# Gate, values and the second half of the output projection with 512 weight columns per matmul instead of 256

## The chip, the cores and the metric

The kernel runs on one core of a Trainium2 chip. The metric is the device time of one execution in microseconds (us), as the median of several runs; all inputs and weights are float32 in device memory. One execution was also taken by the hardware profiler; its rows are what this document reads. Engines are named as in the profile: PE is TensorE's matmul, PEld its load of the stationary operand, DVE is VectorE, ACT ScalarE, POOL GpSimd, SP SyncE, which issues most DMAs.

## What is computed

Two decoder layers on 512 tokens of width 1024. Each layer projects the tokens once, runs two groups of heads side by side, maps both back, adds the residual and normalises, and then runs a gated feed-forward net in the same way. What matters here is the mixer:

```python
proj = x @ w_in[l]
hq, hf, hi, hg, nq, kc, vc, ks, vs, kw, vw, gt = split(proj)
o_a = hgrn2_mixer(hq, hf, hi, hg, ...)      # 4 heads of 128; hi: values, hg: output gate
o_b = nsa_mixer(nq, kc, vc, ks, vs, kw, vw, gt, ...)   # 8 attention heads of 64
mix = concatenate([o_a, o_b], -1) @ w_out[l]
x = layer_norm(ALPHA * x + mix, ln1_g[l], ln1_b[l])
```

In the recurrence `o_a` is a triangular combination of the values of all tokens, normalised per head and multiplied by `hg * sigmoid(hg)`. Values and gate are 512 columns each. The output projection has 1024 rows: the first 512 take `o_a`, the second 512 take `o_b`.

## The kernel before

**Products.** A float32 product is made of three matmuls (`mm3`, L78 to L83): each operand is split into a high part and a rest, and high x high, high x rest and rest x high are summed in a PSUM bank of 512 columns. `load_w` (L53 to L76) fetches a weight of 128x1024 through one of two raw buffers, converts it to the high part on ScalarE (L74) and forms the rest on VectorE (L75). The parts go into pairs of buffers (`wh`, `wl`, three of each), or, by a tag, elsewhere (`a`: one of eleven large buffers).

**Two shapes.** A projection whose result is wanted with features on the partitions (`feats`, L176) has the weight stationary and streams 512 tokens. Gate, values and the output projection are wanted with tokens on the partitions: there the tokens are stationary and the weight columns stream. The first half of the output projection and the down projection do this with 512 columns per matmul, one token tile of 128 to a bank (`wide_mm`, L215). Gate, values and the second half do it with 256 columns, two token tiles to a bank (`tok_mm`, L199); a matmul that opens the second tile of a bank is tied behind the one that opens the bank.

**Gate and values.** `tok256` (L767) makes one quarter of these 1024 columns: two banks with tag `d` (there are two such banks), two weights of 4 k-tiles by 256 columns, and for each of 8 k-tiles and 4 token tiles one `mm3`. ScalarE then copies values (L778), or forms the sigmoid of the gate (L785), which VectorE multiplies by the gate itself (L786). `G` and `V` are large buffers that hold the results.

**The order.** Around the change the order is written out by hand. `layer` first projects what heads 0 and 1 of the recurrence need, then the keys; after these comes the first half of the gate (`tok(1, 0)`, L894 and L895, columns 0 to 255), then the q projections of the first attention heads. Then `nsa_all` runs 16 steps, two for each attention head. After some steps it calls hooks (L898 to L908), whose work gets a priority a little behind the step: projections for heads 2 and 3, the recurrence's levels (`rec`), the second half of the gate after step 4 (`tok(1, 1)`), the values after steps 6 and 7 (`tok(0, 0)`, `tok(0, 1)`), the four outputs of the recurrence (`hg_out`, L426) after step 9, the first half of the output projection after 11 and 12, and the start of the second half after 15. The list scheduler that builds the program fixes each engine's order from priorities and a modelled timeline, so TensorE's queue holds matmuls of these hooks between those of the heads.

**Head outputs.** `hg_out` needs the values of all tokens and works through the single bank with tag `h`: matmuls (L439), squares, norm and gate, transposes (L451). The results are rows 0 to 3 of `Y`, the left operand of the first half (`first_half`, L867), whose result with the residual goes into the rows `R`. Attention heads fill rows 4 to 7 of `Y`.

**The second half.** `second_half` (L884) loads four weights, one for each quarter of 256 output columns, and starts three quarters of the first two token tiles with k 4 to 6. The rest follows after the attention (L921 to L928): for each pair of token tiles and each quarter the last k-tiles, the add onto the rows (L927) and `bn_stats` of 256 columns for each tile (L865). After each pair `norm_turn` normalises the rows and transposes them (L735) for the feed-forward net.

Of the kernel before, what the change touches and what calls it, by code (L numbers as in the profile page):

```python
# [12 lines left out]
AF = mybir.ActivationFunctionType  # L13
OP = mybir.AluOpType
# [20 lines left out]
class Kern:  # L35
# [162 lines left out]

    def tok_mm(self, pts, w, xs, ks, k0, k1, halves=((0, 1),)):  # L199

        for hs in halves:
            for k in ks:
                for t in [2 * h + e for h in hs for e in range(2)]:
                    wh, wl = w(k % 4 * 256, 256)

                    m = self.mm3(pts[t // 2][:, (t % 2) * 256:(t % 2 + 1) * 256], *xs(k, t), wh, wl,
                                 k == k0 and t % 2 == 0, k == k1 and t % 2 == 1)
                    if k == k0:
                        if t % 2 == 0:
                            first = m  # L210
                        else:
                            self.tc.add_manual_dep(m.ins, first.ins.name, mybir.DependencyInfo(
                                mybir.DependencyClass.NoSync, mybir.DependencyReason.DATA), reason="bank start")
# [539 lines left out]
    def layer(self, l):  # L753
# [21 lines left out]
        def take_v(q):  # L775
            def f(b, p):
                with tc.high_priority(offset=500):
                    nc.scalar.copy(self.V[:, 2 * b:2 * b + 2, q * 256:(q + 1) * 256], p)  # L778
            return f

        def take_g(q):
            def f(b, p):
                o = self.G[:, 2 * b:2 * b + 2, q * 256:(q + 1) * 256]
                with tc.high_priority(offset=500):
                    nc.scalar.activation(o, p, AF.Sigmoid)  # L785
                    nc.vector.tensor_tensor(o, p, o, op=OP.mult)  # L786
            return f
# [31 lines left out]
        def tok(which, q):  # L819
            return lambda: tok256(io["wt"][l, which, q], (take_v, take_g)[which](q))  # L820
# [32 lines left out]
        def quart(b, q):  # L853
            return R[b].rearrange("p a b -> p (a b)").rearrange("p (t c) -> p t c", c=1024)[:, :, q * 256:(q + 1) * 256]

# [4 lines left out]
        def v2(p):  # L860
            return p.rearrange("p (t c) -> p t c", c=256)

        def stats(b, q):
            for t in (2 * b, 2 * b + 1):
                nc.vector.bn_stats(self.stats[t][:, q * 6:(q + 1) * 6], rows[t][:, q * 256:(q + 1) * 256])  # L865
# [18 lines left out]
        def second_half():  # L884

            self.stats = [self.small(24, "st", tag="s") for _ in range(NT)]
# [237 lines left out]
def layout(inp):  # L1124
    f = {k: np.asarray(v) for k, v in inp.items()}
    L = DEPTH
# [8 lines left out]
    def tok(m):  # L1135

        k, n = m.shape[1] // 128, m.shape[2] // 256
        return m.reshape(L, k, 128, n, 256).transpose(0, 3, 2, 1, 4).reshape(L, n, 128, k * 256)
# [57 lines left out]
```

## Time and profile before

| | us |
|---|---|
| median of 3 runs | 1354.79 |
| lowest and highest | 1354.45, 1357.82 |
| the profiled execution | 1357.27 |
| its span, first to last instruction | 1355.5 |
| PE busy in the span | 1322.2 |
| DVE busy | 938.9 |
| ACT busy | 718.5 |

The busy time of an engine is the union of its rows. PE's rows overlap, since a matmul starts while the one before is still in the array; what a matmul costs a full queue is the time from its start to the next start. In layer 0 the stretch of the change lies between 76 and 327 us of the span, in layer 1 between 746 and 996. A line number is that of the printed kernel; where a helper issues an operation the line is the helper's, and the names behind it (out<-in) tell whose it is: `ps_d<-whi,xh` with 256 columns is `tok256`, `ps_d<-xh,whi` a projection with the weight stationary.

### The profile page before, as it was taken

The page shows a single profiled execution, that of the slowest core. Times are in us where ns is not written, and L with a number is a line of the kernel's source. Part 1 is how long each engine was busy: PE and PEld are TensorE (multiplying, and loading weights), DVE is VectorE, ACT ScalarE, POOL GpSimd, SP SyncE. Part 2 cuts the span into 40 slices and gives each one's busy share as a digit, 9 for nine tenths or more (in the row PEclk, how much of TensorE's full clock was granted, in tenths as well). Part 3 has the DMA queues.
Part 4 walks back from the last instruction along what each step waited for, and adds up shares of the span by engine and source line. Part 5 has one row for each costly group of instructions (what it writes and reads, how often), then busy time and mean ns, then how long its engine had stood idle before and what let it go on. Part 6 is the DMA issues. An engine that isn't in the chain of part 4 may idle for free.

```text
span 1355.5 us, 23189 instructions
## 1 busy us (share of the span) xinstructions
PE 1322.2 (98%) x8853; PEld 1212.5 (89%) x8853; DVE 938.9 (69%) x1914; ACT 718.5 (53%) x1460; POOL 158.6 (12%) x232
## 2 busy tenths in 40 slices
PE   8999999899999999999999999998999999999996
PEld 6988999789999999888899989987899999998885
DVE  4755898866887777624469468988559777775355
ACT  5254777745565555522543558778265655564131
POOL 1140111110011111000011001111000211100001
PEclk9999999999999999999999999999999999999999
DMA  7252213252177776334534122132513787754344
GB/s 235 79 164 101 78 56 101 55 146 91 63 174 191 180 182 171 102 107 151 191 122 129 65 86 75 55 106 73 154 47 102 181 192 181 181 131 140 94 143 152
DMA packets 61775, 170.26 MB, mean 126 GB/s; under 512 B 7519, under 2 KB 7695, under 8 KB 61152
## 3 DMA queue, kind: packets, MB, share of 16 engines
q1 hardware_dynamic: 44928, 128.93, 29.9%
q0 software_dynamic: 15728, 38.02, 13.4%
q10 hardware_dynamic: 1008, 1.84, 0.4%
q8 instruction: 69, 1.13, 0.3%
q14 instruction: 42, 0.34, 0.1%
HBM read 164.51 MB, written 7.10 MB: 127 GB/s over the span
## 4 chain that ended last, share of the span: by engine, by line
PE 88%; ACT 4%; DMA 3%; DVE 3%; issue 1%; POOL 0%; POOLq 0%; DVEq 0%; ACTq 0%; SPq 0%
PE ps_d L80 16%; PE ps_d L81 15%; PE ps_d L82 15%; PE ps_t L81 4%; PE ps_t L82 4%; PE ps_t L80 4%; PE ps_s L82 4%; PE ps_s L81 4%; PE ps_s L80 4%; PE ps_t L639 2%; DMA wraw<-in_wo 2%; PE ps_h L384 1%; PE ps_o L650 1%; PE ps_o L82 1%; PE ps_o L81 1%; PE ps_o L80 1%
## 5 line engine op out<-in xcount | busy, mean ns | idle before, releaser
L75 DVE TENSOR_TENSOR wlo<-wraw,whi 128x1024 fp32r<-128x1024 f32 (+1 forms) x122 | 149.0, 1221 | 158.2 <-ACT whi L74 157.7
L74 ACT CAST whi<-wraw 128x1024 fp32r<-128x1024 f32 (+1 forms) x122 | 127.5, 1045 | 227.4 <-PE ps_t L82 70.1
L80 PE MATMUL ps_d<-xh,whi 128*128 128x512 f32 (+1 forms) x456 | 154.1, 341 | 3.1 <-ACT gates L490 2.9
L112 ACT CAST whi<-wraw 128x512 fp32r<-128x512 f32 x144 | 89.0, 621 | 124.3 <-PE ps_d L81 93.9
L82 PE MATMUL ps_d<-xh,wlo 128*128 128x512 f32 (+1 forms) x456 | 154.6, 340 | 0.0
L81 PE MATMUL ps_d<-xl,whi 128*128 128x512 f32 (+1 forms) x456 | 154.2, 339 | 0.0
L113 DVE TENSOR_TENSOR wlo<-wraw,whi 128x512 fp32r<-128x512 f32 x144 | 98.4, 689 | 43.4 <-ACT whi L112 39.7
L81 PE MATMUL ps_d<-tl,whi 128*128 128x256 f32 x432 | 121.5, 283 | 0.0
L82 PE MATMUL ps_d<-th,wlo 128*128 128x256 f32 x432 | 120.5, 283 | 0.0
L80 PE MATMUL ps_d<-th,whi 128*128 128x256 f32 x432 | 120.3, 283 | 0.0
L80 PEld LDWEIGHTS ps_d<-xh,whi 128*128 128x128 f32 x456 | 85.8, 190 | 12.3 <-ACT gates L490 3.3
L82 PEld LDWEIGHTS ps_d<-xh,wlo 128*128 128x128 f32 x456 | 86.5, 190 | 8.8
L81 PEld LDWEIGHTS ps_d<-xl,whi 128*128 128x128 f32 x456 | 86.5, 190 | 8.3
L80 PE MATMUL ps_d<-whi,xh 128*128 128x256 f32 (+1 forms) x304 | 90.2, 298 | 0.0
L81 PE MATMUL ps_d<-wlo,xh 128*128 128x256 f32 (+1 forms) x304 | 88.4, 291 | 0.0
L82 PE MATMUL ps_d<-whi,xl 128*128 128x256 f32 (+1 forms) x304 | 87.3, 288 | 0.0
L81 PEld LDWEIGHTS ps_d<-tl,whi 128*128 128x128 f32 x432 | 82.9, 192 | 0.2
L80 PEld LDWEIGHTS ps_d<-th,whi 128*128 128x128 f32 x432 | 82.2, 192 | 0.2
L82 PEld LDWEIGHTS ps_d<-th,wlo 128*128 128x128 f32 x432 | 82.3, 192 | 0.0
L600 ACT ACTIVATE e<-e,mn 128x128 f32<-128x128 f32 (+3 forms) x128 | 71.6, 560 | 13.2 <-DVE mn L598 12.6
L598 DVE CUSTOM_DVE_ANT_0 e<-ps_s,strip 128x128 f32<-128x128 f32 (+3 forms) x128 | 59.2, 484 | 6.8 <-PE ps_s L613 5.9
L643 ACT CAST pth<-ps_t 128x384 fp32r<-128x384 f32 (+1 forms) x96 | 48.8, 510 | 25.9 <-PE ps_t L639 20.8
(482 smaller groups left out, 3957.7 us busy)
## 6 DMA issues: line engine op xcount, KB each, us to landing
wraw<-in_wd SPq DMA_DIRECT2D x59, 512.0 KB, 3.5
wraw<-in_wf SPq DMA_DIRECT2D x31, 512.0 KB, 3.3
wraw<-in_wg SPq DMA_DIRECT2D x26, 512.0 KB, 4.5
wraw<-in_wu SPq DMA_DIRECT2D x26, 512.0 KB, 4.1
ws<-in_wg SPq DMA_DIRECT2D x36, 256.0 KB, 3.5
ws<-in_wg POOLq DMA_DIRECT2D x36, 256.0 KB, 5.2
ws<-in_wu SPq DMA_DIRECT2D x36, 256.0 KB, 3.4
ws<-in_wu POOLq DMA_DIRECT2D x36, 256.0 KB, 4.6
```

Source lines behind the costliest of these rows:

```text
L74: nc.scalar.copy(h, raw[:, i:i + n])
L75: nc.vector.tensor_tensor(o, raw[:, i:i + n], h.bitcast(F32), op=OP.subtract)
L80: first = t.matmul(out, ah, bh, start=start, stop=False, **kw)
L81: t.matmul(out, ah, bl, start=False, stop=False, **kw)
L82: t.matmul(out, al, bh, start=False, stop=stop, **kw)
L112: nc.scalar.copy(h, raw)
L113: nc.vector.tensor_tensor(o, raw, h.bitcast(F32), op=OP.subtract)
L384: nc.tensor.matmul(p2[:, i], S[:, blk(i)], kq(128 * (i + 2), [[2 * w, n], [256 + w, 2], [1, w]]), start=True, stop=True)
L598: nc.vector.tensor_tensor_reduce(out=e, in0=pa, in1=st[:, 512 - pa.shape[-1]:], scale=1.0, scalar=3e38, op0=OP.add, op1=OP.min, accum_out=mn)
L600: nc.scalar.activation(e, e, AF.Exp, bias=mn, scale=-1.0, accum_out=sm)
L639: nc.tensor.transpose(p[:, c:c + 128], E[qt][:, j * 128:(j + 1) * 128], self.ident)
L643: nc.scalar.copy(ph[:, :c], p[:, :c])
```

## The change

`tok256` becomes `tok512`: one call makes all 512 columns of the gate, or of the values. It goes in two passes of two token tiles, each tile with a bank of its own. In the first pass it loads four weights of 2 k-tiles by 512 columns (the first into a large buffer with tag `a`, the other three into the `wh`/`wl` pairs) and uses each for two k-tiles and two token tiles; the second pass uses the same four weights for the other two tiles. With the last weight the tiles go one after the other (`by_tile`). Each tile is then copied, or passed through sigmoid and product, for itself. The whole gate comes after step 4, the whole values after step 6; nothing of the gate stands ahead of the q projections any more. The second half of the output projection has four weights of 2 k-tiles by 512 columns in the same buffers, one token tile to a bank, the add and one `bn_stats` of 512 columns for each tile and half. The weights are laid out for this on the host before the launch.

```diff
-        def tok256(src, consume):
-            pts = [self.ps("d") for _ in range(2)]
-            for i in range(2):
-                w = self.load_w(src[i])
-                self.tok_mm(pts, w, self.xs_of(x), [4 * i + a for a in range(4)], 0, NK - 1, ((0,), (1,)))
+        def tok512(src, consume):
+            ws = []
             for b in range(2):
-                consume(b, pts[b].rearrange("p (t c) -> p t c", c=256))
+                pts = {t: self.ps("d") for t in (2 * b, 2 * b + 1)}
+                for i in range(4):
+                    if b == 0:
+                        ws.append(self.load_w(src[i], tag=None if i else "a"))
+                    self.wide_mm(pts, ws[i], self.xs_of(x), i, i == 0, i == 3, i == 3)
+                for t, p in pts.items():
+                    consume(t, p)
...
+        def take_v(t, p):
+            with tc.high_priority(offset=500):
+                nc.scalar.copy(self.V[:, t], p)
+
+        def take_g(t, p):
+            with tc.high_priority(offset=500):
+                nc.scalar.activation(self.G[:, t], p, AF.Sigmoid)
+                nc.vector.tensor_tensor(self.G[:, t], p, self.G[:, t], op=OP.mult)
...
+        def second_mm(p, c, t, ks):
+            for k in ks:
+                self.mm3(p, *ysf(k, t), *self.wo[c][k // 2 - 2](k % 2 * 512, 512), k == 4, k == 7)
...
-            self.wo = [self.load_w(io["wo"][l, q, 0], tag=t) for q, t in enumerate((("at", 8), ("at", 8), ("f", 3), None))]
-            for q, tag in enumerate("ddh"):
-                early[q] = {0: self.ps(tag)}
-                self.tok_mm(early[q], self.wo[q], ysf, range(4, 7), 4, 7, ((0,),))
+            tags = ((("at", 8), ("at", 8)), (("f", 3), None))
+            self.wo = [[self.load_w(io["wo"][l, c, i], tag=tags[c][i]) for i in range(2)] for c in range(2)]
+            for c, t, tag in ((0, 0, "d"), (0, 1, "d"), (1, 0, "h")):
+                early[c, t] = self.ps(tag)
+                second_mm(early[c, t], c, t, range(4, 7))
...
-        alloc("G")()
-        tok(1, 0)()
         self.feats([feat("nq0"), feat("nq1")], x, lambda i, pt: self.take_q(i, pt))
...
-            4: [(0, rec(3)), (80, tok(1, 1))],
-            6: [(80, nq(3)), (80, alloc("V")), (80, tok(0, 0))],
-            7: [(80, tok(0, 1))],
+            4: [(0, rec(3)), (80, alloc("G")), (80, tok(1))],
+            6: [(80, nq(3)), (80, alloc("V")), (80, tok(0))],
...
-            for q in range(4):
-                pts = early.pop(q, None) if b == 0 else None
-                ks = range(4, 8) if pts is None else [7]
-                pts = pts or {b: self.ps("ddsd"[q] if b else "d")}
-                self.tok_mm(pts, self.wo[q], ysf, ks, 4, 7, ((b,),))
-                nc.vector.tensor_tensor(quart(b, q), v2(pts[b]), quart(b, q), op=OP.add)
-                stats(b, q)
+            for c in range(2):
+                for t in (2 * b, 2 * b + 1):
+                    p = early.pop((c, t), None)
+                    if p is None:
+                        p = self.ps("s" if c else "d")
+                        second_mm(p, c, t, range(4, 8))
+                    else:
+                        second_mm(p, c, t, [7])
+                    o = rows[t][:, c * 512:(c + 1) * 512]
+                    nc.vector.tensor_tensor(o, p, o, op=OP.add)
+                    nc.vector.bn_stats(self.stats[t][:, c * 6:(c + 1) * 6], o)
```

## Rows read from the trace of the kernel before

**Rows 1.** The page: busy time of the engines, granted TensorE clock, last chain by engine.

```profile
PE 1322.2 (98%) x8853; PEld 1212.5 (89%) x8853; DVE 938.9 (69%) x1914; ACT 718.5 (53%) x1460; POOL 158.6 (12%) x232
...
PEclk9999999999999999999999999999999999999999
...
PE 88%; ACT 4%; DMA 3%; DVE 3%; issue 1%; POOL 0%; POOLq 0%; DVEq 0%; ACTq 0%; SPq 0%
```

**Rows 2.** Groups by line and shape, TensorE: count | busy us, mean ns | idle before.

```profile
L80 PE MATMUL ps_d<-whi,xh 128*128 128x256 f32 x256 | 75.5, 296 | 0.0
```

**Rows 3.** Timeline, TensorE, first gate stage: start us, us, instruction.

```profile
89.08 0.28 PE L82 MATMUL ps_d<-whi,xl 128*128 128x256 f32 x1
...
92.44 0.28 PE L80 MATMUL ps_d<-whi,xh 128*128 128x256 f32 x1
```

**Rows 4.** Timeline, TensorE, q projection right behind it.

```profile
103.12 0.39 PE L82 MATMUL ps_d<-xh,wlo 128*128 128x512 f32 x1
...
106.52 0.39 PE L82 MATMUL ps_d<-xh,wlo 128*128 128x512 f32 x1
```

**Rows 5.** Windows: us; busy PE, PEld, DVE, ACT, POOL; clock, DMA share, GB/s.

```profile
148.00:173.00 25.00, 25.00 (x191) 24.12 (x191) 22.84 (x63) 19.74 (x48) 2.96 (x6) 1.00 0.17 54
207.00:230.00 23.00, 23.00 (x185) 22.34 (x184) 21.33 (x64) 16.28 (x40) 1.08 (x2) 1.00 0.23 70
230.00:256.00 26.00, 23.89 (x143) 19.97 (x143) 20.65 (x68) 20.92 (x65) 5.91 (x9) 0.93 0.35 112
256.00:283.00 27.00, 24.47 (x167) 21.60 (x167) 23.88 (x69) 20.41 (x59) 4.55 (x5) 1.00 0.30 73
301.00:327.00 26.00, 24.71 (x203) 23.98 (x201) 19.39 (x41) 11.54 (x17) 1.13 (x2) 1.00 0.37 118
899.00:925.00 26.00, 23.05 (x150) 19.02 (x148) 20.80 (x69) 21.58 (x66) 5.90 (x9) 1.00 0.35 112
925.00:952.00 27.00, 24.47 (x166) 21.64 (x167) 23.86 (x70) 20.48 (x60) 3.89 (x4) 1.00 0.29 69
```

**Rows 6.** Groups by line and shape, VectorE and ScalarE: columns as in rows 2.

```profile
L865 DVE BATCH_NORM_STATS2 st<-r 128x6 f32<-128x256 f32 x32 | 12.0, 416 | 0.1
L1057 DVE BATCH_NORM_STATS2 st<-r 128x6 f32<-128x512 f32 x16 | 10.6, 687 | 0.1
...
L778 ACT COPY v<-ps_d 128x512 f32<-128x512 f32 x8 | 4.6, 580 | 2.5 <-PE ps_d L82 2.5
...
L75 DVE TENSOR_TENSOR wlo<-wraw,whi 128x1024 fp32r<-128x1024 f32 x118 | 144.9, 1228 | 155.0 <-ACT whi L74 154.5
L74 ACT CAST whi<-wraw 128x1024 fp32r<-128x1024 f32 x118 | 123.9, 1050 | 224.8 <-PE ps_t L82 70.1 <-DMA wraw<-in_wd 35.8 <-PE ps_d L81 29.0
```

**Rows 7.** DMA issues: issuer, count, KB each, median us to landing.

```profile
wraw<-in_wt SPq DMA_DIRECT2D x16, 512.0 KB, 3.3
```

**Rows 8.** Timeline of TensorE, ScalarE and VectorE: end of the second gate stage.

```profile
172.50 0.28 PE L82 MATMUL ps_d<-whi,xl 128*128 128x256 f32 x1
...
173.89 1.28 ACT L785 ACT_TABLE_LOAD   x1
...
175.80 1.28 ACT L600 ACT_TABLE_LOAD   x1
...
175.98 0.68 DVE L786 TENSOR_TENSOR g<-ps_d,g 128x512 f32<-128x512 f32 x1
```

**Rows 9.** Timeline, TensorE, transposes behind the second half [idle before <-releaser].

```profile
326.04 0.90 PE L735 MATMUL ps_t<-ident,r 128*128 128x128 f32 x4 [1.21 <-ACT xraw L736]
```

**Rows 10.** Timeline of ScalarE and TensorE: last value copy, first and fourth output.

```profile
230.68 0.58 ACT L778 COPY v<-ps_d 128x512 f32<-128x512 f32 x1
...
235.22 0.39 PE L439 MATMUL ps_h<-v,atd 128*128 128x128 f32 x2
...
271.29 0.39 PE L439 MATMUL ps_h<-v,atd 128*128 128x128 f32 x2
...
278.44 0.66 PE L451 MATMUL ps_h<-ident,hy 128*128 128x128 f32 x4
```

More of the change, by code (lines that the diff above doesn't have):

```diff
@@ L197, in feats @@
                     consume(i, pts[i])
[L199 to L213, printed above, removed]
     def wide_mm(self, pts, w, xs, i, start, stop, by_tile=False):
@@ L817, in alloc, with tok @@
             return f
-        def tok(which, q):
-            return lambda: tok256(io["wt"][l, which, q], (take_v, take_g)[which](q))
+        def tok(which):
+            return lambda: tok512(io["wt"][l, which], (take_v, take_g)[which])
         def hfq(h):
@@ L851, in rblocks @@
             rows.extend(R[t // 2].rearrange("p a b -> p (a b)")[:, (t % 2) * 1024:(t % 2 + 1) * 1024] for t in range(NT))
-        def quart(b, q):
-            return R[b].rearrange("p a b -> p (a b)").rearrange("p (t c) -> p t c", c=1024)[:, :, q * 256:(q + 1) * 256]
         def ysf(k, t):
@@ L858, in ysf @@
             return yh[:, t * 128:(t + 1) * 128], yl[:, t * 128:(t + 1) * 128]
[L860 to L865, printed above, removed]
+        def second_mm(p, c, t, ks):
+            for k in ks:
+                self.mm3(p, *ysf(k, t), *self.wo[c][k // 2 - 2](k % 2 * 512, 512), k == 4, k == 7)
         def first_half(c):
@@ L884, in second_half @@
         def second_half():
-            self.stats = [self.small(24, "st", tag="s") for _ in range(NT)]
-            self.wo = [self.load_w(io["wo"][l, q, 0], tag=t) for q, t in enumerate((("at", 8), ("at", 8), ("f", 3), None))]
-            for q, tag in enumerate("ddh"):
-                early[q] = {0: self.ps(tag)}
-                self.tok_mm(early[q], self.wo[q], ysf, range(4, 7), 4, 7, ((0,),))
+            self.stats = [self.small(12, "st", tag="s") for _ in range(NT)]
+            tags = ((("at", 8), ("at", 8)), (("f", 3), None))
[3 more added lines that the diff above has]
+                second_mm(early[c, t], c, t, range(4, 7))
         self.KHL = (self.big("kh", F32R), self.big("kl", F32R))
         self.feats([feat("ks0"), feat("kw0")], x, lambda i, pt: self.dup_k(i, pt))
-        alloc("G")()
-        tok(1, 0)()
         self.feats([feat("nq0"), feat("nq1")], x, lambda i, pt: self.take_q(i, pt))
@@ L1133, in feat @@
         return w[:, :, c0:c0 + 128].reshape(L, NK, 128, 128).transpose(0, 2, 1, 3).reshape(L, 128, 1024)
-    def tok(m):
-        k, n = m.shape[1] // 128, m.shape[2] // 256
-        return m.reshape(L, k, 128, n, 256).transpose(0, 3, 2, 1, 4).reshape(L, n, 128, k * 256)
-    def tok4(m):
-        t = tok(m)
-        return t.reshape(L, t.shape[1], 128, -1, 1024).transpose(0, 1, 3, 2, 4)
     a["wf"] = np.stack([feat(COLS[n[:2]] + 128 * int(n[2])) for n in FEAT], 1)
-    a["wt"] = np.stack([tok4(w[:, :, 1024:1536]), tok4(w[:, :, 1536:2048])], 1)
     wv = np.concatenate([w[:, :, 2944:3072], w[:, :, 3200:3352]], 2)
     a["wv"] = wv.reshape(L, NK, 128, 280).transpose(0, 2, 1, 3).reshape(L, 128, NK * 280)
-    a["wo"] = tok4(f["w_out"][:, 512:])
     def wide(m):
         return m.reshape(L, -1, 2, 128, 2, 512).transpose(0, 4, 1, 3, 2, 5).reshape(L, 2, -1, 128, 1024)
+    a["wt"] = wide(w[:, :, 1024:2048])
     a["wo1"] = wide(f["w_out"][:, :512])
+    a["wo"] = wide(f["w_out"][:, 512:])
     a["wd"] = wide(f["w_ffn_down"])
```

12 lines of the change are left out of this document (removed).

## Prediction

> **What bounds the kernel now.** I read the page's engine list and clock line first, then the chain that ended last, then TensorE's groups kept apart by shape, then its instructions in order of time, and last the busy times by stage. TensorE is busy 98% of the span, at full granted clock in all 40 slices of the page, and its share of the last chain is 88% [rows 1]; the chain's large parts are the three lines of the split product on the `d` banks. A busy share alone does not say that fewer instructions help, since a matmul's row (296 ns on average for one of 256 columns in gate and values) is longer than the step to the next one [rows 2]. So I take the step from start to start. In a run of 256-column matmuls of the first gate stage there are 28 steps from 89.08 to 92.44: 3.36 us, 120 ns each [rows 3]. In a run of 512-column matmuls right behind it there are 15 steps from 103.12 to 106.52: 3.40 us, 226.7 ns each [rows 4]. Two narrow ones take 240 ns where one wide one takes 226.7, both at full clock. The difference, 13.3 ns for each pair, is a cost per matmul, and it is what the change can remove.
>
> Then I ask stage by stage whether TensorE's queue sets the pace. From 148 to 230 it never stands idle, but VectorE is also busy 22.84 of 25 us and 21.33 of 23 [rows 5]: attention heads run at VectorE's pace and the projections (gate, values, q) fill the holes. From 230 to 283 (899 to 952 in layer 1) the fillers are used up; TensorE idles 2.11, 2.53, 2.95 and 2.53 us of the four windows [rows 5], 10.1 us in all. From 301 to 327, the second half of the output projection, it is busy 24.71 of 26 us [rows 5] and the bound again.
>
> **The change part by part.** (1) *Column width.* Each `tok256` call holds 8 k-tiles x 4 token tiles x 3 products = 96 matmuls; there are four per layer (L895, L901 to L903), 384. The second half holds 4 column quarters x 4 k x 4 tiles x 3 = 192. Over two layers 1152 matmuls of 256 columns become 576 of 512: 1152 x 0.120 = 138.2 us become 576 x 0.2267 = 130.6 us. That is **-7.7 us**, -2.6 per layer in gate and values and -1.3 per layer in the second half. All of it lies on TensorE, which is on the path in these stages.
>
> The Trainium skill ("TensorE: Matmul & The Clock Gate", Back-to-back issue gap) speaks against this: it puts the warm gap at N/2.4 + 2.5 ns. By that rule a pair would save 2.5 ns and the sum would be 576 x 2.5 = 1.4 us, no measurable change. The rows here differ from it, 120 ns for 256 columns and 226.7 for 512, and I go by the rows.
>
> (2) *Evictions* stay as many and as large: eight copies of 128x512 for the values [rows 6] and, by the same loops, eight sigmoids and eight products for the gate, over both layers; afterwards each takes one token tile of 512 columns. The add of the second half keeps its size, and its 32 bn_stats of 256 columns become 16 of 512, at 416 against 687 ns [rows 6]: 13.3 us of VectorE become 11.0, off the path. I count nothing.
>
> (3) *Weights.* Sixteen loads of 512 KB for gate and values before [rows 7], sixteen after; the conversions on ScalarE and VectorE are the same too. What moves is the rhythm. In the first pass over two token tiles a weight serves 12 matmuls, 12 x 0.2267 = 2.7 us, instead of 48 x 0.120 = 5.8 us; in the second pass nothing is loaded. Supply is 3.3 us to landing [rows 7] plus 1.05 and 1.23 us for the two conversions [rows 6], with two raw buffers in turn: (3.3 + 1.05 + 1.23) / 2 = 2.8 us per weight. So without other work TensorE would wait 0.1 us per weight; with attention taking half the stretch it waits for nothing. I count 0; with no cover and a load late by its whole landing, 3.3 us per stage is the bound. On SP's queue the two weight loads of the old first gate stage leave the place ahead of the q loads and go behind the loads of the five hook-2 projections; nobody on that queue waits for longer. The four weights hold one large buffer and all three `wh`/`wl` pairs; the next projection's weight gets a pair when the second pass still has 24 matmuls, 5.4 us, before it, against 2.3 us of conversion.
>
> (4) *Bank handover.* Now a pass ends with the second tile's last six matmuls (`by_tile`), and the next pass writes the first tile's bank right after: 6 x 0.2267 = 1.4 us to empty it. The nearest row for a gate bank is the old one inside attention: its last matmul starts at 172.50 and lasts 0.28, ScalarE gets to it at 173.89, loads a table for 1.28 us, and VectorE's product ends at 176.66 [rows 8], 3.9 us after the matmul. Gap 2.5 us, twice per layer (into the second pass, and into the projection after the gate), 10 us at most over both layers. The old stage had 2.9 us between its two banks (24 matmuls x 0.120). Values have a copy of 0.58 us [rows 6] and no table load, so they fit. What hides the gap is attention's own matmuls, which the queue holds between the fillers in this whole stretch; I take 1 us per layer. Moving the first gate stage among the heads also puts two more sigmoids between exponentials: at most two more pairs of 1.28 us table loads [rows 8], 5.1 us of ScalarE per layer, which has 5.3 and 6.7 us free in the two windows above [rows 5]. I count nothing.
>
> (5) *The move.* 96 matmuls, 11.5 us, leave the front; the q projections and with them the first head start 11.5 us earlier, and 10.9 us of filler are added between the heads. TensorE's work up to the last value column stays the same, so that point moves by -2.6 us only, unless heads that run ahead take TensorE time before it (rival below) or the fillers reach into the idle tail (other rival). I count 0.
>
> (6) *End of the second half.* The first rows of a token pair are now complete 12 matmuls (2.7 us) ahead of the second, so the norm of one tile starts earlier; the transposes that follow wait 1.21 us for ScalarE now [rows 9], and the two layers could gain 2.4 us at most. I take 1 us per layer, against the 1 us of (4).
>
> Sum: -7.7 us. The profiled execution took 1357.3 us (1355.5 of span and 1.8 around it), so 1349.6 on its scale; it is 2.5 us above the median of the three timed runs, 1354.8. On the median's scale: **1347.1 us**.
>
> **The rivals.** *The idle tail fills (faster).* If the heads keep their 11.5 us lead and the fillers last longer, the 10.1 us in which TensorE idles after them [rows 5] go: 1347.1 - 10.1 = 1337.0. For it: the heads start earlier and the fillers do not end earlier than by 2.6 us. Against: the idle lies in the softmax chain of the last heads, which have no other work to wait for.
>
> *Banks or gaps eat it (no change).* The full 10 us of (4) give 1354.8 - 7.7 + 10.0 = 1357.1. For it: VectorE is at 92% there, so an eviction queues. Against: matmuls of attention lie between the fillers. A second way to no change is that the columns alone count, and a wide matmul between those of attention steps by twice 120 ns: nothing is saved, 1354.8; the run of 15 steps [rows 4] speaks against it. The Trainium skill's gap rule (part 1) would give nearly the same, 1353.4.
>
> *Values land later (slower).* The four head outputs run one after the other through a single `h` bank once the values are there: the last value copy starts at 230.68, the first output's matmuls at 235.22, the fourth's at 271.29, its transposes at 278.44 [rows 10]: 12 us for each. And the first half of the output projection needs all four. If heads with an 11.5 us lead take their share ahead of the values, this chain starts late. The fillers of the 82 us from 148 to 230 are three stages of 96 and one q projection of 24 matmuls, 288 x 0.120 + 24 x 0.2267 = 40.0 us, so heads and levels take 51%: 11.5 x 0.51 = 5.9 us ahead of the last value column, against 2.6 saved. The handover's 1 us lies ahead of the values too, and the gain of (6) I leave out here, since its row can stay as it is: 5.9 - 2.6 + 1.0 - 1.3 = +3.0 per layer, 1354.8 + 6.0 = 1360.8. (The share could be 0 to all of the 11.5.) It decides from the point where the last value copy is later than 230.68 by more than the second half gives back, and the outputs keep their 12 us. Against: with fewer heads left the outputs would queue less.
>
> **How the numbers follow.** Forecast 0.50, with a range of its own of 1343 to 1351; idle tail filled 0.14; no change 0.18 (0.03 of it that columns alone count); slower 0.18. A measurement of this kernel tells about 0.3%, 4.1 us, from no change: faster is under 1350.7, slower over 1358.9. Nine tenths of the forecast's case lie under 1350.7 (0.45), with the filled tail 0.59; 0.05 + 0.18 = 0.23 the same; 0.18 slower. The range goes from the upper half of the filled tail to just past the slow case: 1338 to 1362. One unknown belongs in it: the granted clock is 0.93 from 230 to 256 and 1.00 in layer 1's like window [rows 5], so part of that window ran at the lower of the two levels, 1.2 instead of 2.4 GHz; 26 x 0.07 = 1.8 us of clock that may come or go.
>
> **What would show it.** Step 1: 576 matmuls of 512 columns at 226 to 228 ns apart in place of 1152, TensorE's count down by 576. Step 4: idle ahead of `d` matmuls released by the gate's product on VectorE, and how many table loads the gate has. Step 5: when the last value copy lands against 230.68 in layer 0, and TensorE's idle from there to 283 [rows 5, 10]. Step 6: idle before the transposes. The prediction is wrong if the steps save as computed but the time does not follow: then the tail, from the last value column to the second half, has become longer than the 70 us that it takes now (231 to 301).

## The result: 1386.2 us against 1356.2, and the profile after

The changed kernel takes 1386.21 us (median of five runs, 1384.06 to 1390.20) beside 1356.17 for the kernel before (five runs, 1354.45 to 1357.82: the three of the table above and two more): the ratio is 1.0229, with a 95% interval of 1.0216 to 1.0243. It is 30 us slower where 7.7 us less was forecast, and 24 us above the upper end of the range. The profiled execution took 1384.06 us with a span of 1382.3, which is 26.8 more than the profiled execution of before.

The page of the kernel after, engines and last chain (it answers to [rows 1]):

```profile
PE 1334.8 (97%) x8277; PEld 1184.6 (86%) x8277; DVE 933.1 (68%) x1898; ACT 718.4 (52%) x1460; POOL 156.8 (11%) x232
...
PE 80%; DVE 9%; DMA 4%; ACT 3%; issue 2%; POOL 1%; POOLq 0%; SPq 0%; DVEq 0%; ACTq 0%
```

TensorE has 576 matmuls fewer (8853 - 8277), as computed. VectorE's share of the last chain rose from 3% to 9%, although VectorE has slightly less to do: more of what sets the end now waits for it. TensorE in the gate stage of layer 0, timeline, first and last of a run of 512-column matmuls (as [rows 4]):

```profile
173.90 0.39 PE L81 MATMUL ps_d<-wa,xh 128*128 128x512 f32 x1
...
177.76 0.39 PE L80 MATMUL ps_d<-whi,xh 128*128 128x512 f32 x1
```

Between them lie 17 steps, 3.86 us, 227 ns each. So the width does what was said of it, and the loss is elsewhere. Busy time by stage, layer 0 (columns as in [rows 5]; the second line starts where the gate starts):

```profile
135.00:169.00 34.00, 29.64 (x173) 22.85 (x172) 33.46 (x103) 24.68 (x65) 6.53 (x14) 1.00 0.10 32
169.00:207.00 38.00, 37.13 (x189) 30.65 (x188) 24.43 (x60) 24.17 (x50) 3.44 (x7) 1.00 0.26 89
207.00:230.00 23.00, 23.00 (x118) 19.43 (x116) 9.15 (x27) 9.70 (x21) 1.07 (x2) 1.00 0.20 69
```

From 135 to 169 VectorE is busy 33.46 of 34 us and TensorE idles 4.36: heads and levels of the recurrence alone, with no projection between them. From 207 to 230 it is the other way round: TensorE never idles and VectorE does 9.15 of 23 us, where it did 21.33 [rows 5]: mostly projections. Work that ran side by side now runs one after the other. The starts of TensorE's instructions say the same in one sum: the time from each start to the next, less a step for its columns (120 ns at 256, 227 at 512, others on the straight line through these two), adds up to about 34 us from 125 to 350 before and to about 49 after. That is 15 more, less the 3.9 that the width saves in a layer, 11; the feed-forward net's first activation (its table load) came 11.4 us later, at 365.10 instead of 353.67.

Why did no projection run from 135 to 169? ScalarE's timeline of the kernel after, the conversion of the gate's first weight and the instruction right before it:

```profile
167.86 0.62 ACT L651 CAST y<-yv 128x512 fp32r<-128x512 f32 x1
168.39 1.04 ACT L74 CAST wa<-wraw 128x1024 fp32r<-128x1024 f32 x1
```

SP's queue, issues of weight loads, from 105 to 178 (the first line holds four issues, the first at 109.48, the last at 131.21):

```profile
109.48 22.06 SPq L58 DMA_DIRECT2D wraw<-in_wt  x4
139.66 0.33 SPq L58 DMA_DIRECT2D wraw<-in_wf  x1
173.30 0.33 SPq L58 DMA_DIRECT2D wraw<-in_wt  x1
```

The four loads of `in_wt` are the gate's weights. The conversion at 168.39 waits for the semaphore of the load issued at 109.48, which landed at 112.91: the gate's first weight lay in its raw buffer for 55 us, while the other three went through the second raw buffer into the `wh`/`wl` pairs. It was converted half a microsecond behind the first write of `y`, the result of the first two attention heads. From 139.66 the second raw buffer was taken too, by a weight of the next projection, and SP issued nothing for 33.6 us. ScalarE was busy right up to the conversion and its row names no wait, so the trace shows the order of its queue: the conversion had its place behind `y`. On TensorE the last matmul of the projections before the gate starts at 135.86 and the first one of the gate at 169.48:

```profile
135.86 0.39 PE L82 MATMUL ps_d<-xh,wlo 128*128 128x512 f32 x1
...
169.48 0.74 PE L80 MATMUL ps_d<-wa,xh 128*128 128x512 f32 x2
```

In layer 1 the pair is there again, `y` at 851.38 and `wa` at 851.91.

### The profile page after: what moved, and what is told of

Read it like the earlier page. It is cut to its first block, busy times and chain, and to the rows that moved or that the text cites. A ratio compares the mean times of both kernels' runs of the same rounds, so it can differ in the third digit from the quotient of the medians.

```text
span 1382.3 us, 22029 instructions
## 1 busy us (share of the span) xinstructions
PE 1334.8 (97%) x8277; PEld 1184.6 (86%) x8277; DVE 933.1 (68%) x1898; ACT 718.4 (52%) x1460; POOL 156.8 (11%) x232
## 4 chain that ended last, share of the span: by engine, by line
PE 80%; DVE 9%; DMA 4%; ACT 3%; issue 2%; POOL 1%; POOLq 0%; SPq 0%; DVEq 0%; ACTq 0%
PE ps_d L80 15%; PE ps_d L81 14%; PE ps_d L82 14%; PE ps_t L82 4%; PE ps_t L81 4%; PE ps_t L80 4%; PE ps_s L80 4%; PE ps_s L82 4%; PE ps_s L81 4%; DVE e L582 1%; DMA wraw<-in_wg 1%; PE ps_t L623 1%; DMA wraw<-in_wf 1%; PE ps_s L495 1%; DVE ptl L628 1%
## 5 line engine op out<-in xcount | busy, mean ns | idle before, releaser
L74 ACT CAST whi<-wraw 128x1024 fp32r<-128x1024 f32 (+1 forms) x118 | 123.3, 1045 | 226.1 <-PE ps_t L82 66.6
L75 DVE TENSOR_TENSOR wlo<-wraw,whi 128x1024 fp32r<-128x1024 f32 (+1 forms) x118 | 143.9, 1220 | 143.3 <-ACT whi L74 141.2
L584 ACT ACTIVATE e<-e,mn 128x256 f32<-128x256 f32 (+3 forms) x128 | 71.8, 565 | 20.6 <-DVE mn L582 19.8
L582 DVE CUSTOM_DVE_ANT_0 e<-ps_s,strip 128x256 f32<-128x256 f32 (+3 forms) x128 | 58.9, 484 | 9.7 <-PE ps_t L623 5.4
L628 DVE TENSOR_TENSOR ptl<-ps_t,pth 128x384 fp32r<-128x384 f32 (+1 forms) x96 | 55.9, 594 | 2.9 <-ACT pth L627 2.8
L82 PE MATMUL ps_s<-xh,wlo 128*128 128x256 f32 (+1 forms) x192 | 55.9, 292 | 1.7 <-DVE wlo L75 1.7
L81 PE MATMUL ps_s<-xl,whi 128*128 128x256 f32 (+1 forms) x192 | 55.8, 292 | 0.0
```

Source lines behind the costliest of these rows:

```text
L74: nc.scalar.copy(h, raw[:, i:i + n])
L75: nc.vector.tensor_tensor(o, raw[:, i:i + n], h.bitcast(F32), op=OP.subtract)
L81: t.matmul(out, ah, bl, start=False, stop=False, **kw)
L82: t.matmul(out, al, bh, start=False, stop=stop, **kw)
L582: nc.vector.tensor_tensor_reduce(out=e, in0=pa, in1=st[:, 512 - pa.shape[-1]:], scale=1.0, scalar=3e38, op0=OP.add, op1=OP.min, accum_out=mn)
L584: nc.scalar.activation(e, e, AF.Exp, bias=mn, scale=-1.0, accum_out=sm)
```

## Experiments

All times are medians; each kernel stands beside runs of the kernel before on the same chip. Ratios are to that, with 95% intervals. The clock is the granted TensorE clock of a kernel's runs, on average (in brackets that of the kernel before).

| run | what it is | us | before | ratio | clock |
|---|---|---|---|---|---|
| e1 | after, heads' buffer first | 1361.94 | 1355.38 | 1.0042 (1.0027 to 1.0056) | 0.9926 (0.9962) |
| e6 | before, one gate weight in the large buffer | 1375.65 | 1355.38 | 1.0147 (1.0128 to 1.0166) | 0.9955 (0.9962) |
| e2 | before, wide second half only | 1365.27 | 1355.38 | 1.0069 (1.0052 to 1.0086) | 0.9910 (0.9962) |
| e4 | after, old second half | 1378.96 | 1355.38 | 1.0173 (1.0151 to 1.0194) | 0.9958 (0.9962) |
| e5, e19 | e4, heads' buffer first | 1355.69, 1355.51 | 1355.73, 1355.01 | 1.0001 (0.9990 to 1.0012), 1.0012 (1.0000 to 1.0023) | 0.9969 (0.9963), 0.9961 (0.9964) |
| e7 | e2, tiles in turns | 1358.18 | 1355.73 | 1.0019 (1.0003 to 1.0034) | 0.9945 (0.9963) |
| e9 | e1, tiles in turns | 1360.48 | 1355.73 | 1.0034 (1.0023 to 1.0045) | 0.9937 (0.9963) |
| e10 | after, gate ahead of the heads | 1389.71 | 1355.73 | 1.0251 (1.0233 to 1.0270) | 0.9850 (0.9963) |
| e14 | e2, norm behind evictions | 1359.90 | 1354.09 | 1.0049 (1.0032 to 1.0066) | 0.9940 (0.9970) |
| e11 | e9, norm behind evictions | 1360.57 | 1354.09 | 1.0051 (1.0032 to 1.0069) | 0.9925 (0.9970) |
| e12, e18 | before, gate moved, heads' buffer first | 1352.97, 1354.30 | 1354.09, 1355.01 | 0.9991 (0.9979 to 1.0002), 0.9989 (0.9977 to 1.0001) | 0.9965 (0.9970), 0.9955 (0.9964) |
| e13 | before, wide values only | 1367.04 | 1354.09 | 1.0097 (1.0078 to 1.0117) | 0.9952 (0.9970) |
| e15 | before, heads' buffer first | 1355.58 | 1355.77 | 0.9998 (0.9989 to 1.0007) | 0.9963 (0.9967) |
| e16 | e13, heads' buffer first | 1363.36 | 1355.77 | 1.0058 (1.0044 to 1.0071) | 0.9945 (0.9967) |
| e17 | e12, gate wide | 1357.51 | 1355.77 | 1.0018 (1.0006 to 1.0030) | 0.9939 (0.9967) |

**The order of the buffers.** The weight `wa` and the heads' result `y` both come from `big`, a tag of 11 buffers. The theory: a tag's buffers are handed out in the order in which the program first names their tenants. The gate is written behind the second head's end in the program, so its weight gets no buffer before `y` has one, however early it lands, and its conversion is queued behind `y`. The rival was that the two losses come from the 512-column matmuls themselves. e1 takes the heads' buffer before the heads:

```diff
+        self.Y[2] = self.big("y", F32R)
+        nc.gpsimd.memset(self.Y[2][:, 0, :1].bitcast(F32), 0.0)
         self.nsa_all({
```

> The changed kernel with one addition: the large buffer of Y[2] is taken and one of its columns is set to zero (a small memset on GpSimd) ahead of the attention loop. Theory A (the gate's first weight cannot have its large buffer before Y[2], whose first use stands earlier in the program, has its own): the first gate matmul in layer 0 moves from 169.5 to about 137 us, TensorE's time lost from start to start between 125 and 175 us falls from 18 to about 5 us per layer, and the time to 1348 to 1360 us (about 13 us per layer less). Theory B (the rhythm of the two passes: four weights in a burst, banks emptied too late, the first gate half moved among the heads): nothing of that depends on Y[2], the time stays at 1380 to 1390 us.

e6 is the opposite: the kernel before, unmoved and with 256 columns, where one weight of the gate's second half is put into the large buffer.

```diff
-                w = self.load_w(src[i])
+                w = self.load_w(src[i], tag=None if i else tag)
...
+            return lambda: tok256(..., "a" if (which, q) == (1, 1) else None)
```

> The kernel before with one edit: the first weight of its second gate stage (after step 4) goes into a large buffer, as in the changed kernel; shape, order and number of matmuls stay. Theory A: that stage, which begins at 147.6 us in layer 0, cannot begin before Y[2] is first written at the end of the second head (about 165 to 185), TensorE is left without filler meanwhile, and the time rises by 8 to 14 us per layer, to 1372 to 1384. Theory B: no change, within 3 us of before.

ScalarE in e1: the weight is converted as soon as it has landed (116.50), and `y` comes 65 us behind it.

```profile
116.53 1.05 ACT L74 CAST wa<-wraw 128x1024 fp32r<-128x1024 f32 x1 [2.48 <-DMA wraw<-in_wt]
...
181.43 0.61 ACT L651 CAST y<-yv 128x512 fp32r<-128x512 f32 x1
```

ScalarE in e6:

```profile
182.28 0.62 ACT L667 CAST y<-yv 128x512 fp32r<-128x512 f32 x1
182.80 1.04 ACT L74 CAST wa<-wraw 128x1024 fp32r<-128x1024 f32 x1
```

TensorE's first gate matmul in e1:

```profile
139.78 0.39 PE L80 MATMUL ps_d<-wa,xh 128*128 128x512 f32 x1
```

It comes 29.7 us earlier than in the kernel after. e1 takes 1.9 of the 2.3% away; e6 puts 1.5% into a kernel that has nothing else of the change. A control tells whether taking the buffer early is worth something by itself:

> A control: the kernel before with nothing changed but that the heads' buffer is taken ahead of the heads. If taking it early is worth nothing by itself, the time stays within 0.3% of the kernel before (1351.5 to 1359.5 us). If it falls by more, part of what e1, e5 and e12 gained is due to this and not to the wait of the weights that it took away.

It is not (0.9998). So the wait is the cause of some 25 us of the 30 (1.0229 - 1.0042 = 0.0187, times 1355). With the old second half the same edit takes 1.7% away (e4 against e5). What the traces do not show is how the buffers are assigned; they show the sequence, and that it goes when the order of first use is turned round.

**The second half has a loss of its own.** e2 and e4 split the change in two.

> The kernel before with the second half of the output projection alone at 512 columns. By the step from start to start (120 against 226.7 ns): -1.3 us per layer, 1353.5, both theories. If the wide second half itself causes the later transposes at its end (idle of 2.4 us before them and some 6 us of loss per layer behind 325 us in the changed kernel), the time rises by about 8 us instead, to 1364.

> The changed kernel with the old second half (256 columns): gate and values alone. Theory A: all of the loss is here and the late end of attention also costs the end of the second half its cover, so 1386 plus the 2.6 us of the narrow second half, 1389. If the wide second half has a loss of its own at its end (some 5 us per layer), 1376.

The wide second half alone loses 9.9 us where 4.6 were to be gained (1.3 of issue and 1 of the earlier norm, per layer), and gate and values lose the rest. ScalarE in e2 at the end of layer 0's second half: L727 is the norm of one token tile, L736 an eviction of its transposes.

```profile
317.19 2.43 ACT L727 ACTIVATE r<-r,nb,rstd 128x1024 f32<-128x1024 f32 x2 [3.80 <-DVE nb L726]
322.60 1.24 ACT L727 ACTIVATE r<-r,nb,rstd 128x1024 f32<-128x1024 f32 x1
323.86 1.02 ACT L736 ACTIVATE xraw<-ps_t,lnt 128x256 f32<-128x256 f32 x2
325.21 0.56 ACT L736 ACTIVATE xraw<-ps_t,lnt 128x256 f32<-128x256 f32 x1 [0.33 <-PE ps_t L735]
326.09 1.24 ACT L727 ACTIVATE r<-r,nb,rstd 128x1024 f32<-128x1024 f32 x1 [0.32 <-DVE nb L726]
```

ScalarE in the kernel before, same place:

```profile
318.54 2.49 ACT L727 ACTIVATE r<-r,nb,rstd 128x1024 f32<-128x1024 f32 x2 [4.42 <-DVE nb L726]
323.26 1.02 ACT L736 ACTIVATE xraw<-ps_t,lnt 128x256 f32<-128x256 f32 x2 [2.23 <-PE ps_t L735]
...
329.34 1.24 ACT L727 ACTIVATE r<-r,nb,rstd 128x1024 f32<-128x1024 f32 x1 [0.49 <-DVE nb L726]
331.00 1.24 ACT L727 ACTIVATE r<-r,nb,rstd 128x1024 f32<-128x1024 f32 x1
```

Two norms come first in both. Before, all evictions that TensorE needed for its next steps came ahead of the second pair's norms (329.34, 331.00). In e2 the third tile is complete early, and its norm (322.60) stands in ScalarE's queue ahead of the first eviction, the fourth's (326.09) ahead of the fourth. TensorE in e2, the transposes that wait for an eviction:

```profile
324.48 1.14 PE L735 MATMUL ps_t<-ident,r 128*128 128x128 f32 x4 [2.69 <-ACT xraw L736]
325.82 0.69 PE L735 MATMUL ps_t<-ident,r 128*128 128x128 f32 x2 [0.20 <-ACT xraw L736]
327.83 0.69 PE L735 MATMUL ps_t<-ident,r 128*128 128x128 f32 x2 [1.32 <-ACT xraw L736]
```

They wait 4.2 us where they waited 1.21 [rows 9]. e7 computes the two tiles of a pair in turns, so that both are complete together again:

```diff
-                for t in (2 * b, 2 * b + 1):
-                        second_mm(p, c, t, range(4, 8))
+                for k in range(4, 8):
+                    for t, p, kk in zip(ts, ps, ks):
+                        if k in kk:
+                            second_mm(p, c, t, [k])
```

> The kernel before with the wide second half alone (as e2), but the two token tiles of a pair are computed in turns, chunk by chunk, so that both banks of a pair end together, as they did before. Theory (in e2 the third tile was ready early and its normalisation of 1.24 us stood in ScalarE's queue ahead of the evictions on which TensorE's transposes wait): the norms fall back behind the first three evictions, TensorE's idle time at the transposes falls from 5.1 us to under 2.5 in the first layer, and the time to 1355 to 1359 us from 1365. Rival (the loss lies elsewhere, as in the changed order of instructions in the second normalisation of the layer, between 650 and 720 us): 1362 us or more.

e14 leaves the matmuls as in e2 and only forbids the norm to stand ahead of the fourth eviction:

```diff
+            if b and not which:
+                self.tc.add_manual_dep(m.ins, self.ev[3].ins.name, ...)
```

> The kernel before with the wide second half alone (as e2), and one order more: the normalisations of the second token pair may not stand in ScalarE's queue ahead of the fourth eviction of the first pair's transposes. The matmuls keep e2's order, tile after tile. Theory (the place of that norm in ScalarE's queue is what e2 lost): 1356 to 1360 us, like e7, against e2's 1365. Rival (e7 gained from computing the tiles in turns, not from the queue): 1363 us or more.

e7 takes 0.50 of the 0.69% away. The transposes wait 1.75 us there, as they do in e14 (1.55 and 0.20 in both). TensorE in e7:

```profile
321.52 0.90 PE L735 MATMUL ps_t<-ident,r 128*128 128x128 f32 x4 [1.55 <-ACT xraw L736]
```

e14 takes 0.20, less than expected and not clear of noise (its interval overlaps that of e2). So the norm's place makes the transposes wait; that it alone is what e7 gains is not shown, since e7 also reorders TensorE's matmuls. ScalarE in e14:

```profile
323.08 1.02 ACT L740 ACTIVATE xraw<-ps_t,lnt 128x256 f32<-128x256 f32 x2
324.00 1.23 ACT L727 ACTIVATE r<-r,nb,rstd 128x1024 f32<-128x1024 f32 x1
325.13 0.60 ACT L743 CAST xh<-xraw 128x512 fp32r<-128x512 f32 x1
```

TensorE in e14:

```profile
325.79 0.65 PE L80 MATMUL ps_d<-xh,whi 128*128 128x256 f32 x2 [1.20 <-ACT xh L743]
```

The norm now stands in front of the conversion that the feed-forward net's first matmul needs, and TensorE waits 1.20 us for that: the wait has moved to the next user of the same queue. The last 0.2% of e7 is not settled by a run; one place is the layer's last norm, where TensorE waits for VectorE's half of a weight. In e7:

```profile
685.98 0.53 PE L82 MATMUL ps_s<-xh,wlo 128*128 128x256 f32 x1 [2.19 <-DVE wlo L75]
```

In the kernel before:

```profile
687.09 0.39 PE L82 MATMUL ps_s<-xh,wlo 128*128 128x256 f32 x1 [0.47 <-DVE wlo L75]
```

TensorE comes there earlier and waits longer: 1.7 us of the gain are given back in code that the change did not touch.

Part of all this is the granted TensorE clock, and the expectations did not ask for it. Windows of e2 (columns as in [rows 5], the clock behind POOL):

```profile
317.00:324.00 7.00, 4.78 (x24) 3.70 (x22) 5.41 (x14) 4.76 (x5) 1.09 (x2) 1.00 0.11 43
324.00:331.00 7.00, 5.00 (x20) 3.82 (x21) 2.68 (x6) 5.81 (x11) 0.55 (x1) 0.52 0.23 75
```

The kernel before, the later of the two:

```profile
324.00:331.00 7.00, 5.71 (x46) 5.00 (x45) 4.79 (x12) 6.31 (x11) 1.64 (x2) 1.00 0.27 78
```

e7:

```profile
324.00:331.00 7.00, 7.00 (x61) 7.00 (x60) 2.84 (x8) 5.66 (x9) 0.55 (x1) 1.00 0.15 60
```

In e2 nearly this whole window ran at the lower of the two levels, 1.2 instead of 2.4 GHz, after one in which TensorE was busy 4.78 of 7 us; its 256-column matmuls step 210 to 220 ns between 330.21 and 330.85 and 120 ns from 331.22 on. In layer 1 the clock is 0.51 from 1000 to 1007. In e14 it is 0.76 from 324 to 331, in e7 0.57 from 686 to 690, where TensorE waits for the weight. Since the lower level is half the upper one, the share of the clock that is missing beyond that of the kernel before, times the span, estimates what the clock can have cost at most: 7.1 us of e2's 9.9, 4.1 of e14's 5.8, 2.4 of e7's 2.5. What makes the clock fall was not tested.

**Both mended.** e5 and e9 put the parts together, and e11 adds e14's order to e9.

> The kernel after with two edits: the buffer that the heads fill first is taken ahead of the heads (as in e1), and the second half of the output projection is the old one with 256 columns. Theory (two separate losses, the order of the buffers and the wide second half): e1 less the 9.9 us that the wide second half cost by itself, so about 1352 us, 3 to 4 us below the kernel before, because the narrower issue of gate and values (some 5 us by the sum of the prediction) is then no longer eaten. Rival (the gate and value stages lose something of their own besides the buffer): 1357 us or more.

> The kernel after with the heads' buffer taken ahead of the heads (e1) and the second half's tiles computed in turns (e7). Theory (both named losses are causes, and they add): e1's 1362 less what e7 takes off e2, about 1351 to 1355 us, so at or below the kernel before. Rival (the second half's loss is not the norm's place in ScalarE's queue): about 1362 us, like e1.

> The kernel after with the heads' buffer taken first, the second half's tiles in turns (as e9), and the same order on ScalarE as in e14. In e9 the third tile's norm stood ahead of the second eviction again in the second layer, and the layer's first feed-forward activation came 5.2 us later than in e5 (2.3 of it were there when the layer began). Theory: the remaining 3 us fall away, about 1357 us. Rival (the second layer's loss in e9 is of another kind): 1360 us or more.

All three miss what the sum of the named losses asks for. e5 comes out even with the kernel before (3 to 4 us less expected), e9 gains 0.1% on e1 (0.5% expected, and the intervals overlap), and e11 gains nothing on e9. So the two causes do not simply add. By the same estimate the clock is 3.5 us of the 4.8 that e9 still loses and 6.1 of e11's 6.5; e5 has no such loss and its gain is missing all the same, so gate and values lose something besides the buffer.

**Where gate and values lose.** e12 moves the gate without widening anything, e10 puts the wide gate ahead of the heads, e13 widens the values alone; e16 and e17 widen values or gate with the heads' buffer taken first.

```diff
-        alloc("G")()
-        tok(1, 0)()
...
-            4: [(0, rec(3)), (80, tok(1, 1))],
+            4: [(0, rec(3)), (80, alloc("G")), (80, tok(1, 0)), (80, tok(1, 1))],
```

> The kernel before with the gate moved and nothing widened: all four quarters of gate and values keep 256 columns, the gate's first half stands between the heads next to its second, and the heads' buffer is taken first. It is e5 without the wider matmuls. If the width of gate and values is worth its issue time (5.1 us over both layers) and the move costs as much, this gives about 1361 us. If the move is free, as the prediction counted it, this gives 1355.5 us and the width of gate and values brought nothing in e5.

> The kernel after with the whole gate stage put ahead of the heads, where no buffer of the heads stands before its weights; values and second half as in after. Theory (the 20 to 24 us are the wait for the buffer behind the heads): the wait is gone and the time falls to 1358 to 1372 us; the wide second half's 10 us remain, and the heads start about 23 us later than in after with less to fill their gaps. Rival (the gate's own 512-column form costs the time, wherever it stands): 1380 us or more.

```diff
-            6: [(80, nq(3)), (80, alloc("V")), (80, tok(0, 0))],
-            7: [(80, tok(0, 1))],
+            6: [(80, nq(3)), (80, alloc("V")), (80, values)],
```

> The kernel before with the values alone widened to 512 columns; the gate and the second half as before, nothing moved. By issue time alone 2.6 us less over both layers: 1353 us. Theory (the order of the buffers is harmless here, because the heads' buffer is in use before the values begin): 1351 to 1356 us. Rival (a value stage of twice the length, both banks held to its end, makes the heads wait): 1358 us or more.

> The kernel before with the values alone widened (as e13) and the heads' buffer taken ahead of the heads. In e13 the values' first weight was cast 0.5 us behind the first write of the heads' buffer. Theory (that wait is the whole loss of e13, 13 us): 1351 to 1355 us, since the narrower issue takes 2.6 us off. Rival (the value stage in 512 columns loses something of its own): 1358 us or more.

> The kernel of e12 (gate whole between the heads, heads' buffer first, all with 256 columns) with the gate alone widened to 512. Theory (the issue time is gained where nothing waits): 2.6 us less than e12, about 1350 to 1352 us, so below the kernel before by 0.2 to 0.4%. Rival (the gate's longer steps lose in the second layer what they gain in the first, as e5 did against e12): 1354 us or more.

The move is free: e12 is 0.1% under the kernel before, e18 repeats it, and both intervals hold 1. e10's number is that of its rival, but the trace gives another reason: the buffer again, now for the values. No run of e10 with the heads' buffer first tells how much of its loss that is. ScalarE in e10:

```profile
201.38 0.62 ACT L651 CAST y<-yv 128x512 fp32r<-128x512 f32 x1 [0.36 <-DVE yv L648]
201.91 1.04 ACT L74 CAST wa<-wraw 128x1024 fp32r<-128x1024 f32 x1
```

(5.1 us more stand ahead of its gate's first matmul in front, for a bank that VectorE still reads; that was not followed up.) For e13 I had held the order harmless, since `y` is in use before the values begin. It is in use just then, and the pair is there a fifth time. ScalarE in e13:

```profile
187.11 0.62 ACT L667 CAST y<-yv 128x512 fp32r<-128x512 f32 x1 [0.21 <-DVE yv L664]
187.64 1.04 ACT L74 CAST wa<-wraw 128x1024 fp32r<-128x1024 f32 x1
```

Taking the buffer early gives back 0.4 of e13's 1.0% (e16, where the weight is converted at 146.20, 0.9 us after it landed), and 0.6 stay. That is not the price of wide values as such: with the gate moved and wide they cost nothing (e17 has narrow values and is at 1.0018, e5 and e19 have wide ones and are at 1.0001 and 1.0012). What e16 loses with the gate's first half in its old place stays open (7.6 us, of which the clock can be 3.0). The gate's wide form alone costs 0.3% (e17 at 1.0018, e12 at 0.9991), of which the clock can be 0.2 (0.9939 against 0.9965). The wide form is more than the width: it also goes in two passes and holds four weights at once, and no run separates these. e18 and e19 are e12 and e5 again, side by side.

> The kernel of e12 again (gate whole between the heads, heads' buffer first, 256 columns throughout), with more rounds, beside e19 on the same chip. If the move gains something, the ratio to the kernel before stays below 0.999 with its whole interval; if it is free, the interval holds 1.

> The kernel of e5 again (as e18, and gate and values with 512 columns). Theory (the issue time saved by the width, 5.1 us, is lost to waits in the tail of the heads, where less matmul work is left to fill them): no faster than e18, by 0 to 3 us slower. Rival (the width is worth its issue time, and e5 against e12 was scatter between chips): 4 to 5 us below e18.

The wide one is no faster, and 0.2% slower if anything; the clock is no reason here (0.9961 against 0.9955). Busy time by stage in layer 1, the heads' tail, in e18:

```profile
895.00:920.00 25.00, 24.08 (x169) 21.62 (x168) 19.08 (x65) 21.21 (x66) 4.76 (x7) 1.00 0.30 105
```

And in e19:

```profile
895.00:920.00 25.00, 21.66 (x134) 17.48 (x133) 21.84 (x71) 18.63 (x58) 6.40 (x10) 1.00 0.33 106
```

With the wide stages the last value copy of layer 1 ends at 890.0 instead of 902.8, and TensorE idles 3.34 instead of 0.92 us from 895 to 920, with VectorE busier: the fillers end sooner and the heads have less beside them. The last head's last products start at 968.7 instead of 945.0. The order of the work differs, so the two lines do not hold the same work, and the 2.4 us are a reading, not a test. The layers differ too: in these two profiled executions the feed-forward net's first table load comes 0.9 us earlier with the wide form in layer 0 (350.02 against 350.91) and 3.8 us later in layer 1 (1020.96 against 1017.19). What in the wide form takes the saved issue away stays open.

## Why the prediction was wrong

**(1) Column width** held as an issue cost: 576 matmuls fewer, 227 ns a step against the 226.7 taken. The Trainium skill ("TensorE: Matmul & The Clock Gate", Back-to-back issue gap) gives N/2.4 + 2.5 ns, 215.8 at 512 columns, for a matmul by itself, and about 131 ns for a stream of weight loads and matmuls; the prediction took the first for a stream. This case's trace disagrees with both, after the change as before it. But "all of it lies on TensorE, which is on the path in these stages" failed for gate and values: with the buffer's wait gone and the wide form as the only difference, the 5.1 us do not appear (e19 against e18). It fits that a stage in which VectorE is busy 21 of 23 us [rows 5] is not shortened by shortening its filler; no run shows this by itself. The rival that banks or gaps eat it, 1357.1, is near where e5 lands, but only as a number: see (4).

**(2) Evictions** and bn_stats behaved as computed and stayed off the path.

**(3) Weights: the step that failed most.** It says "the four weights hold one large buffer and all three `wh`/`wl` pairs" and counts 0, with 3.3 us per stage as bound. It asked how fast weights come and who gets the pairs next, and never when the large buffer may be taken. The weight waited 55 us in its raw buffer, and SP's queue 33.6 us with it ("nobody on that queue waits for longer" failed too). Its price is 25 us of the 30. That a gate weight needed another buffer than before stood in the diff, and eleven buffers of one tag with their order of first use in the code.

The Trainium skill ("Perfetto Trace Analysis", Optimization Strategy) says that a gap repeated over a stretch can mean that the next tile finds no memory to be allocated. Here a tile did come late, but no gap of TensorE says so. Its waits in the kernel after from 135 to 169, total, times and longest:

```profile
PE ps_h L368 <- DVE atm L373: 1.6, 3, 0.8
PE ps_o L634 <- DVE ptl L628: 1.0, 4, 0.3
```

These two and the three shorter ones of that list are waits of the heads and the recurrence. None names the weight, since the order of TensorE's queue already had the gate behind it.

**(4) Bank handover** cost nothing that shows: between 110 and 340 no wait of TensorE's `d` matmuls is put down to the gate's product or a value copy. The two passes have two pairs of table loads per layer.

**(5) The move** was rightly counted at 0 (e12, e18). What it was combined with was not: in the kernel after, the last value copy of layer 0 starts at 238.07 instead of 230.68 [rows 10]. The rival "values land later" had this sign, and a delay of 4.3 us for 7.4 measured. Its mechanism was another: heads did run ahead (the second head's last matmuls at 163.3 instead of 182.7), but because no filler could start, not by taking their share. What the prediction named as its sign of being wrong, a longer tail, did not come. The last row of the first half on VectorE, before:

```profile
303.20 0.68 DVE L879 SCALAR_TENSOR_TENSOR r<-xr,ps_d 128x512 f32<-128x512 f32 x1
```

And after:

```profile
310.58 0.68 DVE L855 SCALAR_TENSOR_TENSOR r<-xr,ps_d 128x512 f32<-128x512 f32 x1
```

From the last value copy that is 72.5 us in both (the prediction's 70 end at a window's edge, 301). Of layer 0's 11.4 us, 7.4 were lost ahead of the last value copy and 4.0 behind the first half.

**(6) End of the second half** was counted at -1 us per layer and went the other way. The early norm was seen, but as a gain at most: its place in ScalarE's queue, ahead of the evictions that TensorE waits for, was not asked. The step and the width together were to give -4.6 us; e2 measured +9.9, of which e7 removes 7.

**The clock** stands in the range alone, with 1.8 us. The page's 9 stands for 90% or more, so it does not say "full granted clock in all 40 slices"; the 0.93 of [rows 5] lies in these slices. The five runs of the kernel after have 0.990 on average, the profiled execution of before 0.996: at most 9 us of the 30, by the estimate above. The price of the buffer is not the clock's: e4 loses 1.7% at 0.9958 against 0.9962.

**The range** took in a wait bounded at 3.3 us per stage. A buffer that is refused until another tenant has it is bounded by that tenant's time, not by a load's: here 55 us.

## To carry to other kernels

When a change gives an operand another buffer, ask what stands before it in the order of first use of that tag, and when the last of these tenants is first written: in the traces here the operand came no earlier, whenever its load had landed. When one tile of a pair is made ready earlier, look up what its next step gets ahead of on its in-order engine. And do not count on shortening the filler of a stage that another engine paces: here it gave nothing back.

## What was not expected of the hardware

A wait can be invisible on the engine where it costs most: TensorE's idle of 4.36 us from 135 to 169 lies in small waits, most of them for VectorE, and the weight's lateness shows only as SP's 33.6 us without an issue, as the 55 us between a landing and its conversion, and as the 0.53 us between two conversions. And a wait may be followed by a slower stretch: behind the idle time at the transposes of e2 the granted clock was 0.52 for 7 us, behind the shorter one of e7 it was 1.00. Beyond that the runs showed nothing of the chip that rows of before had not shown: 227 ns per step at 512 columns, 1.28 us per table load, 3.4 us from issue to landing for the gate's first weight.
